# Block products of a feed-forward layer on one core: the split of the next pair's weight sums placed behind the copies of this pair's partial sums on ScalarE

## The chip, the cores and the metric

The kernel runs on one core of a Trainium2 chip. The metric is the device time of one execution in microseconds (us). Three runs of the kernel before took 1837.56, 1838.80 and 1840.89 us, median 1838.8. The core's engines work side by side, each through its own list of instructions in order: TensorE (PE, matmuls; PEld its weight loads), VectorE (DVE), ScalarE (ACT), GpSimd (POOL) and SyncE (SP, which here only issues DMA transfers). They wait for each other on semaphores.

## The reference

The kernel computes a trunk of two layers on 512 tokens of width 1024. Each layer has three attention mixers in parallel, a gated merge, and a feed-forward part; the modulation (shift, scale, gate) comes from a condition vector `c` by a product with `w_ada`.

```python
for l in range(DEPTH):
    mod = (cond @ w_ada[l] + b_ada[l]).reshape(b, 6, d)
    sh_a, sc_a, gt_a, sh_f, sc_f, gt_f = [mod[:, i, None, :] for i in range(6)]
    ...
    u = rms_norm(x, g_ffn[l]) * (1 + sc_f) + sh_f
    h = jax.nn.silu(u @ w_ffn_gate[l]) * (u @ w_ffn_up[l])
    x = x + gt_f * (h @ w_ffn_down[l])
return rms_norm(x, g_final)
```

All is float32. `D_FF` is 2816, that is 22 columns of 128. The change lies in the line that makes `h`.

## The kernel before, in words

**Split products.** TensorE multiplies in a short float format (`fp32r`). Each operand is split into a high part (a cast on ACT) and a low part (source less high part, on DVE), and every product is three matmuls: high by high, high by low, low by high (helper `mm3`, lines 225 to 227). So all weights pass from HBM into a raw tile (`wraw`, four buffers, line 173, issued by SP), through ACT's cast (line 196 for whole tiles `wh`, line 269 in `split`) and DVE's subtraction (line 198 for `wl`, line 270 in `split`).

**Pairs of block products.** Gate and up columns `f` = 0 to 2 are plain products. For `f` = 3 to 21 the two columns of a pair are cut into 2 x 2 blocks and computed by seven block products instead of eight, from sums of weight blocks and sums of activation blocks (`t1` to `t4`, made once). Each product is 12 matmuls of 256 columns. There are 19 such pairs in each of the two layers. TensorE's order is fixed by hand, and in pair `f` it is:

- y2 (`t2` by the pair's s24 sum, onto `y`), v1 (`t1` by s31, into `v`), p1 of the next pair (into the next `y`), y3 (`t3` by s31, onto `y`), v2 (onto `v`, by s24), p2 of the next pair (into `z`), y4 (`t4` by the plain weights, onto `y`).

`y`, `v` and `z` are PSUM tiles. Between products ACT copies the partial sum out: `kept_copy` (line 1035) makes the copy of `y` after p1 ("y1"), of `y` after y2 ("y2") and of `v` after v1 ("v1"). y3 goes on writing `y` and so waits for the y2 copy; v2 waits for the v1 copy; the next y2 waits for the y1 copy. y4 waits for DVE's sum u22 (line 1082), which reads `y` after y3.

**Weights of a pair.** A pair's weights are two raw tiles: `ra` (four blocks) and `rb`. `plain(f)` casts `ra` whole (`wh`) and half of `rb` (`a12h`), and fetches further loads. `sums(f)` adds blocks: s31 on DVE (line 1015), s24 in two sums on POOL (lines 1016 and 1017). `summed(f, i)` splits a sum: i = 0 gives s31h and s31l, i = 1 gives s24h and s24l. When the last reader of a raw tile is done, SP may issue the load that comes next in its order into that buffer.

**Background.** While the pairs run in layer 0, each odd pair asks for one `background` step: one column block of the next layer's `w_ada` is loaded into a `wraw` buffer and reduced against the condition vector by DVE (line 399). There are ten in layer 0 and one in layer 1. A finished pair's `h` column is stored to HBM (`h_kept`, line 930, issued by POOL) and read back for the down product.

**What sets the order.** On PE the order is as written. On ACT, DVE, POOL and SP a scheduler places the instructions by priority: recorded earlier means more urgent, and what stands under `high_priority` is taken as 30 steps more urgent. An order dependency without a semaphore (`add_manual_dep`) puts an instruction behind another on its engine.

The functions that the change touches, with the lines that the profile names:

Of the kernel before, what the change touches and what calls it, by code (L numbers as in the profile page):

```python
# [24 lines left out]
NF = FF // P  # L25
# [43 lines left out]
def tile_hybrid_trunk(ctx: ExitStack, tc: tile.TileContext, xT, cvec, pos, cst, cmask, vec, gfin,  # L69
                      w_ada, w_first, w_proj, w_uq, w_uqr, w_ukv, w_o, w_out, w_gu, w_dn, out):  # L70
    nc = tc.nc
    act, dve, pool, pe = nc.scalar, nc.vector, nc.gpsimd, nc.tensor
# [16 lines left out]
    def pst(tag, name):  # L89
        return ps.tile([P, S], F32, tag=tag, bufs=PB[tag], name=name)  # L90
# [6 lines left out]
    order = mybir.DependencyInfo(mybir.DependencyClass.NoSync, mybir.DependencyReason.SCHED_ONLY)  # L97
# [7 lines left out]
    def fn(*args, **kw):  # L105
        i = act.activation(*args, **kw).ins  # L106
        tc.add_manual_dep(i, phase["fence"].name, order, reason="table set")
        phase["now"].append(i)
# [67 lines left out]
    def fetch(r):  # L176
        while len(raws) < min(r, cap[0]):
            raws.append(load(*LOADS[len(raws)][1:]))
# [3 lines left out]
    def divide(want, after=None):  # L182

        while len(splits) < min(want, cap[0]):
            j = len(splits)
            fetch(j + 1)
            c = LOADS[j][2]
            p_, tag = wp, ""
            if LOADS[j][0][0] == "h":
                p_, tag = hroom[0], f"h{LOADS[j][0][2]}"  # L190
            elif fourth[0]:
                fourth[1] += 1
                if fourth[1] % 4 == 1:
                    p_, tag = fourth[0], "x"
            wh = p_.tile([P, D], F32R, tag="wh" + tag, name="wh")
            ins = [act.copy(wh[:, :c], raws[j][:, :c]).ins]  # L196
            wl = p_.tile([P, D], F32R, tag="wl" + tag, name="wl")
            ins.append(dve.tensor_sub(wl[:, :c], raws[j][:, :c], wh[:, :c].bitcast(F32)).ins)  # L198
            for i, a in zip(ins, after or ()):
                tc.add_manual_dep(i, a.name, order, reason="more urgent")  # L200
            splits.append((wh, wl))
# [62 lines left out]
        for _ in g:  # L264
            tick()

    def split(h, l, src, scale=None):
        if scale is None:
            act.copy(h, src)  # L269
            dve.tensor_sub(l, src, h.bitcast(F32))  # L270
        else:
            act.activation(h, src, AF.Copy, scale=scale)
            dve.scalar_tensor_tensor(l, src, scale, h.bitcast(F32), ALU.mult, ALU.subtract)
# [141 lines left out]
    def background(n):  # L415
        for _ in range(n):
            if pending:
                ada(*pending.pop(0))
# [4 lines left out]
    def values(ap, psv, name, got):  # L423

        vt = ap.tile([P, S], F32, tag="vt", name="vt" + name)
        act.copy(vt, psv)

        def rest():
            t = pst("mm", "vT" + name)
            for b in range(NB):  # L430
                pe.transpose(t[:, b * P : (b + 1) * P], vt[:, b * P : (b + 1) * P], identf)
            v = ap.tile([P, NB, 2, 2, 64], F32R, tag="vv", bufs=2, name="v" + name)
            tv = t.rearrange("p (b h f) -> p b h f", b=NB, h=2)
            split(v[:, :, :, 0], v[:, :, :, 1], tv)
            got.append(v)

        later(3, rest)
# [80 lines left out]
    for l in range(L):  # L518
# [32 lines left out]
        if l == 0:  # L551
            table(LN_EXP)
            st = su.enter_context(scoped("start"))
            t = pst("pt", "ssa0")
# [27 lines left out]
            def sums(c, after):  # L582
                return [ada(0, i, c, wada[c][i], i == 0, after[i]) for i in range(2)][1]
# [244 lines left out]
        for res, raw_, g0, tag in ((ckv, lat[3:], V_GKV, "ckv"), (cq, lat[:3], V_GQ, "cq")):  # L828
            for b in norms(tag + str(l), len(raw_) * P, latp):
# [4 lines left out]
                for i, t in enumerate(raw_):  # L834
                    rw, h, lo = t[:, b.cols], res[i][0][:, b.cols], res[i][1][:, b.cols]
# [9 lines left out]
        for w in range(1, 13):  # L845
# [12 lines left out]
            for a in range(2):  # L858
                h = 2 * w - 2 + a
# [17 lines left out]
        with scoped(f"mo{l}", "right") as op:  # L877
# [11 lines left out]
            for m in range(KC - NL):  # L889
                t = pst("mm", "wout")  # L890
# [6 lines left out]
            for b, tag in zip(both, ("mm", "s")):  # L897
                for i, w in enumerate(ws):
                    t = pst(tag, "wout")[:, :H]
# [29 lines left out]
        def kept(f, g):  # L929
            pool.dma_start(out=hsave[f], in_=g)  # L930
# [44 lines left out]
        for f in range(1, NSTD):  # L975
            if f == 1:
                t = ts[2]
            else:
                t = pst("mm", "fg")
# [14 lines left out]
        def half(hl, i):  # L994
            return [tuple(w[:, i * HC + k * P : i * HC + (k + 1) * P] for w in hl) for k in range(4)]

        def plain(f):

            j = first_of["ra", l, 2 * f]
            divide(j + 1)  # L1000
            fetch(j + 2)
            RA[f] = splits[j]
            h, lo = (gs.tile([P, HC], F32R, tag="a12" + a, bufs=2, name="a12" + a) for a in "hl")
            split(h, lo, raws[j + 1][:, HC:])
            A12[f] = h, lo
            splits.append(None)
# [10 lines left out]
            pool.tensor_add(s24[:, 1], s24[:, 0], rb[:, HC:])  # L1017
            sraw[f] = s31, s24

        def summed(f, i):  # L1020
            src = sraw[f][i].rearrange("p a c -> p (a c)")
            nm_ = ("s31", "s24")[i]
            h, lo = (gs.tile([P, D], F32R, tag=nm_ + a, bufs=1 + i, name=nm_ + a) for a in "hl")
            split(h, lo, src)
            SW[f, i] = h, lo

        def product(o, wt, acts, start):
            for k, ((wh, wl), (ah, al)) in enumerate(zip(wt, acts)):
                mm3(o, wh, wl, ah, al, start and k == 0, k == 3, not start)
# [2 lines left out]

        def kept_copy(name, src):
            t = gs.tile([P, H], F32, tag=name, name=name)
            act.copy(t, src)
            return t

        def p1(f):
            Y[f] = pst("mm", "y")[:, :H]
            product(Y[f], half(RA[f], 0), B[0, 0], True)  # L1040
            with tc.high_priority(offset=HP):
                Y1[f] = kept_copy("y1", Y[f])

        def p2(f):
            z = pst("s", "z")[:, :H]
            product(z, half((A12[f][0], A12[f][1]), 0), B[1, 0], True)
            G[f] = tp.tile([P, S], F32, tag="g", bufs=3, name="g")
            with tc.high_priority(offset=HP):
                dve.tensor_add(G[f][:, HALVES[0]], z, Y1[f])

        plain(NSTD)
        sums(NSTD)
        summed(NSTD, 1)
        summed(NSTD, 0)
        plain(NSTD + 1)
        p1(NSTD)
        p2(NSTD)
        for f in range(NSTD, NF):
            if f + 1 < NF:
                sums(f + 1)  # L1060
                summed(f + 1, 1)
            if f + 2 < NF:
                plain(f + 2)
            if f == NF - 1:
                at[0] = first_of["h", l, 0]
                cap[0] = first_of["h", l, 2]
                divide(cap[0])
            background(f % 2)
            y_, g = Y[f], G[f]
            product(y_, half(SW[f, 1], 0), TB["t2"], False)  # L1070
            with tc.high_priority(offset=HP):
                y2c = kept_copy("y2", y_)
            v = pst("pt", "v")[:, :H]
            product(v, half(SW[f, 0], 1), TB["t1"], True)
            with tc.high_priority(offset=HP):
                v1 = kept_copy("v1", v)
            if f + 1 < NF:
                p1(f + 1)
            product(y_, half(SW[f, 0], 0), TB["t3"], False)
            with tc.high_priority(offset=HP):  # L1080
                u22 = gs.tile([P, H], F32, tag="u22", name="u22")
                dve.tensor_add(u22, y_, v1)
            if f + 1 < NF:
                summed(f + 1, 0)
                fetch(first_of["ra", l, 2 * NSTD] + 2 * (f - NSTD) + 7)
            product(v, half(SW[f, 1], 1), B[1, 1], False)
            with tc.high_priority(offset=HP):
                dve.tensor_add(g[:, HALVES[1]], v, y2c)
                fn(g, g, AF.Silu)
            if f + 1 < NF:  # L1090
                p2(f + 1)
            product(y_, half(RA[f], 1), TB["t4"], False)
            with tc.high_priority(offset=HP):
                ga, gb = g[:, HALVES[0]], g[:, HALVES[1]]
                dve.scalar_tensor_tensor(gb, u22, -1.0, gb, ALU.mult, ALU.mult)
                dve.scalar_tensor_tensor(ga, y_, -1.0, ga, ALU.mult, ALU.mult)
                kept(f, g)
# [41 lines left out]
        for m in range(2, KC - 1):  # L1139
            t = pst("mm", "dn")  # L1140
# [6 lines left out]
        for b, tag in zip(both, ("mm", "s")):  # L1147
            t = pst(tag, "dn")[:, :H]
# [117 lines left out]
def _build(arrays):  # L1266
    import concourse.bacc as bacc

    nc = bacc.Bacc("TRN2", target_bir_lowering=False, num_devices=1)
    feeds, args = {}, []  # L1270
    for name, a in arrays.items():
        feeds[f"in_{name}_dram"] = a
        args.append(nc.dram_tensor(f"in_{name}_dram", a.shape, mybir.dt.from_np(a.dtype), kind="ExternalInput").ap())
    args.append(nc.dram_tensor("out_dram", (KC, P, S), F32, kind="ExternalOutput").ap())
    with tile.TileContext(nc) as tc:
        tile_hybrid_trunk(tc, *args)
    return nc, feeds
# [10 lines left out]
```

## Time and profile before

| | before |
|---|---|
| runs, us | 1837.56, 1838.80, 1840.89 |
| median, us | 1838.8 |
| profiled execution, its own time, us | 1839.1 |
| its span, us | 1837.3 |
| mean granted TensorE clock | 0.991 |
| PE busy, us (share of the span) | 1790.6 (97%) |
| DVE busy, us | 1398.3 (76%) |
| ACT busy, us | 965.5 (53%) |
| POOL busy, us | 281.0 (15%) |
| DMA, mean GB/s over the span | 135 |

The span is the time from the first to the last instruction in the profiled execution; the execution's own time is 1.8 us longer. Times in the trace count from the span's start. The block products of layer 0 lie at about 620 to 815 us, those of layer 1 at about 1517 to 1708. A row of the timeline gives start, duration, engine, line, operation and tiles, and in brackets how long the engine was idle before and what released it. Layer 0's pairs start at 619.66 (pair 3), 633.62 (pair 4), 643.30 (pair 5) and 653.13 (pair 6).

### The profile page before, as it was taken

The page shows a single profiled execution, that of the slowest core. Times are in us where ns is not written, and L with a number is a line of the kernel's source. Part 1 is how long each engine was busy: PE and PEld are TensorE (multiplying, and loading weights), DVE is VectorE, ACT ScalarE, POOL GpSimd, SP SyncE. Part 2 cuts the span into 40 slices and gives each one's busy share as a digit, 9 for nine tenths or more (in the row PEclk, how much of TensorE's full clock was granted, in tenths as well). Part 3 has the DMA queues.
Part 4 walks back from the last instruction along what each step waited for, and adds up shares of the span by engine and source line. Part 5 has one row for each costly group of instructions (what it writes and reads, how often), then busy time and mean ns, then how long its engine had stood idle before and what let it go on. Part 6 is the DMA issues. An engine that isn't in the chain of part 4 may idle for free.

```text
span 1837.3 us, 27818 instructions
## 1 busy us (share of the span) xinstructions
PE 1790.6 (97%) x10324; PEld 1552.4 (84%) x10324; DVE 1398.3 (76%) x2301; ACT 965.5 (53%) x1751; POOL 281.0 (15%) x398
## 2 busy tenths in 40 slices
PE   6999999999999999999999999999999999999997
PEld 4788888888889899988887887888888889999887
DVE  8888887778756899976568898877776588898533
ACT  4767884454335455553237688645433374555521
POOL 4122100001000233210002121000110013332000
PEclk8999999999999999999999999999999999999999
DMA  7423223434652455568644233343455324445631
GB/s 281 146 78 73 82 72 121 118 113 142 205 164 74 126 159 159 165 200 281 203 139 113 54 82 82 92 123 113 131 184 179 120 87 132 144 128 166 212 97 46
DMA packets 86263, 247.52 MB, mean 135 GB/s; under 512 B 11824, under 2 KB 15024, under 8 KB 86128
## 3 DMA queue, kind: packets, MB, share of 16 engines
q1 hardware_dynamic: 75120, 224.83, 39.5%
q0 software_dynamic: 11008, 20.92, 4.0%
q8 instruction: 81, 1.33, 0.3%
q14 instruction: 54, 0.44, 0.1%
HBM read 220.74 MB, written 15.73 MB: 129 GB/s over the span
## 4 chain that ended last, share of the span: by engine, by line
PE 78%; DVE 9%; DMA 5%; ACT 4%; issue 3%; POOL 1%; DVEq 0%; SPq 0%; ACTq 0%; POOLq 0%
PE gate L225 5%; PE gate L226 5%; PE gate L227 5%; PE proj L225 5%; PE proj L226 4%; PE proj L227 4%; PE y L225 3%; PE y L226 3%; PE y L227 3%; DMA wraw<-in_w_ada_dram 3%; PE o L225 2%; PE o L227 2%; PE o L226 2%; PE dn L226 2%; PE dn L225 2%
## 5 line engine op out<-in xcount | busy, mean ns | idle before, releaser
L196 ACT CAST wh<-wraw 128x1024 fp32r<-128x1024 f32 (+4 forms) x316 | 294.2, 934 | 317.3 <-PE dn L226 72.0
L198 DVE TENSOR_TENSOR wl<-wraw,wh 128x1024 fp32r<-128x1024 f32 (+4 forms) x316 | 362.3, 1150 | 119.2 <-ACT wh L196 112.9
L225 PE MATMUL proj<-uh,wh 128*128 128x512 f32 x384 | 161.1, 420 | 0.2
L225 PE MATMUL gate<-uh,wh 128*128 128x512 f32 x384 | 153.4, 400 | 0.0
L226 PE MATMUL proj<-ul,wh 128*128 128x512 f32 x384 | 151.2, 394 | 0.0
L227 PE MATMUL proj<-uh,wl 128*128 128x512 f32 x384 | 151.1, 393 | 0.0
L226 PE MATMUL gate<-ul,wh 128*128 128x512 f32 x384 | 150.2, 391 | 0.0
L227 PE MATMUL gate<-uh,wl 128*128 128x512 f32 x384 | 150.2, 391 | 0.0
L225 PE MATMUL dn<-wh 128*128 128x512 f32 (+1 forms) x396 | 145.1, 366 | 0.0
L226 PE MATMUL dn<-wl,wh 128*128 128x512 f32 (+1 forms) x396 | 145.0, 366 | 0.0
L227 PE MATMUL dn<-wh,wl 128*128 128x512 f32 (+1 forms) x396 | 144.8, 366 | 0.0
L399 DVE CUSTOM_DVE_ANT_0 wraw<-wraw,condb 128x1024 f32<-128x1024 f32 x80 | 97.5, 1219 | 48.0 <-DMA wraw<-in_w_ada_dram 48.0
L1016 POOL TENSOR_TENSOR s<-s,wraw 128x512 f32<-128x512 f32 x38 | 49.3, 1298 | 246.5 <-ACT a12h L269 166.8
L227 PEld LDWEIGHTS proj<-uh,wl 128*128 128x128 f32 x384 | 72.4, 188 | 16.7
L227 PEld LDWEIGHTS gate<-uh,wl 128*128 128x128 f32 x384 | 72.1, 188 | 15.9
L226 PEld LDWEIGHTS dn<-wl,wh 128*128 128x128 f32 x396 | 74.7, 189 | 12.6 <-DVE wl L198 0.7
L227 PEld LDWEIGHTS dn<-wh,wl 128*128 128x128 f32 x396 | 74.7, 189 | 12.3 <-DVE wl L198 0.2
L225 PEld LDWEIGHTS dn<-wh 128*128 128x128 f32 x396 | 74.7, 189 | 12.2
L225 PEld LDWEIGHTS gate<-uh,wh 128*128 128x128 f32 x384 | 72.2, 188 | 12.9
L226 PEld LDWEIGHTS gate<-ul,wh 128*128 128x128 f32 x384 | 72.3, 188 | 12.5
L106 ACT ACTIVATE lefts<-ss 128x512 f32<-128x512 f32 (+1 forms) x64 | 28.1, 439 | 100.5 <-DVE ss L450 85.6
L225 PEld LDWEIGHTS proj<-uh,wh 128*128 128x128 f32 x384 | 72.7, 189 | 9.1 <-PE sm L746 0.8
(443 smaller groups left out, 5364.5 us busy)
## 6 DMA issues: line engine op xcount, KB each, us to landing
wraw<-in_w_proj_dram SPq DMA_DIRECT2D x96, 512.0 KB, 3.7
wraw<-in_w_gu_dram SPq DMA_DIRECT2D x88, 512.0 KB, 3.7
wraw<-in_w_ada_dram SPq DMA_DIRECT2D x80, 512.0 KB, 3.5
wraw<-in_w_dn_dram SPq DMA_DIRECT2D x32, 512.0 KB, 4.3
wraw<-in_w_o_dram SPq DMA_DIRECT2D x48, 256.0 KB, 2.6
h_kept<-g POOLq DMA_DIRECT2D x44, 256.0 KB, 5.0
wraw<-h_kept SPq DMA_DIRECT2D x22, 512.0 KB, 4.9
wada<-in_w_ada_dram SPq DMA_DIRECT2D x16, 512.0 KB, 5.4
```

Source lines behind the costliest of these rows:

```text
L106: i = act.activation(*args, **kw).ins
L196: ins = [act.copy(wh[:, :c], raws[j][:, :c]).ins]
L198: ins.append(dve.tensor_sub(wl[:, :c], raws[j][:, :c], wh[:, :c].bitcast(F32)).ins)
L225: pe.matmul(o, wh, ah, start=start, stop=False, skip_group_check=again)
L226: pe.matmul(o, wh, al, start=False, stop=False, skip_group_check=again)
L227: pe.matmul(o, wl, ah, start=False, stop=stop, skip_group_check=again)
L399: ins = dve.tensor_tensor_reduce(out=wt, in0=wt, in1=condb, op0=ALU.mult, op1=ALU.add, scale=1.0, scalar=0.0, accum_out=m).ins
L1016: pool.tensor_add(s24[:, 0], s31[:, 1], ra[:, :HC])
```

## The change

`split` gets an argument `after`: an instruction behind which ACT's cast is placed by an order dependency. `kept_copy` records its copies in a list. In the loop over the pairs, the split of the next pair's s24 sum (`summed(f + 1, 1)`) and the plain weights of the pair after (`plain(f + 2)`) are recorded no longer at the start of the pair but behind the copy of v1, and the split's cast is tied behind that copy. `background(f % 2)` stays where it was and so is now recorded ahead of `plain(f + 2)`.

```diff
-    def split(h, l, src, scale=None):
+    def split(h, l, src, scale=None, after=None):
         if scale is None:
-            act.copy(h, src)
+            i = act.copy(h, src).ins
+            if after:
+                tc.add_manual_dep(i, after.name, order, reason="more urgent")
             dve.tensor_sub(l, src, h.bitcast(F32))
...
-        def summed(f, i):
+        def summed(f, i, after=None):
...
-            split(h, lo, src)
+            split(h, lo, src, after=after)
             SW[f, i] = h, lo
...
         def kept_copy(name, src):
             t = gs.tile([P, H], F32, tag=name, name=name)
-            act.copy(t, src)
+            copies.append(act.copy(t, src).ins)
             return t
+
+        copies = []
...
         for f in range(NSTD, NF):
             if f + 1 < NF:
                 sums(f + 1)
-                summed(f + 1, 1)
-            if f + 2 < NF:
-                plain(f + 2)
             if f == NF - 1:
...
             with tc.high_priority(offset=HP):
                 v1 = kept_copy("v1", v)
+            if f + 1 < NF:
+                summed(f + 1, 1, copies[-1])
+            if f + 2 < NF:
+                plain(f + 2)
             if f + 1 < NF:
                 p1(f + 1)
```

The order on TensorE is the same in both programs. The other engines differ in the two feed-forward stages alone. The lines of the changed kernel are up to five higher: 1035 becomes 1037, 270 becomes 272, 399 becomes 401, 1082 becomes 1087.

On ACT, pair 4 of layer 0. The copies read y2's `y`, v1's `v` and p1's `y`, in this order. Before:

```order
L106 ACTIVATE g<-g 128x512
L269 CAST a12h<-wraw 128x512
L196 CAST wh<-wraw 128x1024
L269 CAST s24h<-s_6446 128x1024
L1035 COPY y_6476<-y 128x256
L1035 COPY v_6491<-v 128x256
L1035 COPY y_6506<-y 128x256
L269 CAST s31h<-s_6445 128x1024
```

and with the change:

```order
L106 ACTIVATE g<-g 128x512
L269 CAST a12h<-wraw 128x512
L196 CAST wh<-wraw 128x1024
L1037 COPY y_6462<-y 128x256
L1037 COPY v_6477<-v 128x256
L269 CAST s24h<-s_6446 128x1024
L1037 COPY y_6506<-y 128x256
L269 CAST s31h<-s_6445 128x1024
```

The cast of the s24 sum moved from ahead of the copies of y2 and v1 to behind both. In the first pair of a layer the cast `a12h` stands between the two copies, and the cast `wh` of `ra` of pair 5 ahead of the copy of p1's `y`, before and now.

On SP, the loads of layer 0's feed-forward stage, from its start: six plain tiles (`f` = 0 to 2), then `ra` and `rb` of pairs 3, 4, 5 and so on, and the ada columns. Before:

```order
L173 DMA wraw<-in_w_gu_dram 128x1024 x12
L173 DMA wraw<-in_w_ada_dram 128x1024
L173 DMA wraw<-in_w_gu_dram 128x1024 x4
L173 DMA wraw<-in_w_ada_dram 128x1024
L173 DMA wraw<-in_w_gu_dram 128x1024 x4
```

and with the change:

```order
L173 DMA wraw<-in_w_gu_dram 128x1024 x10
L173 DMA wraw<-in_w_ada_dram 128x1024
L173 DMA wraw<-in_w_gu_dram 128x1024 x5
L173 DMA wraw<-in_w_ada_dram 128x1024
L173 DMA wraw<-in_w_gu_dram 128x1024 x4
```

The first ada column moved ahead of the two loads of pair 5; the next ones stand between `ra` and `rb` of pairs 7, 9 and so on, and no longer ahead of an `ra`.

On DVE, pair 4 of layer 0. `ISA wraw,mod_81` is the reduction of an ada column, `u_` is u22, `L1015` and `L1017` the s31 sum. Before, this pair had no ada column (pair 5 had, at the same place):

```order
L198 TENSOR_TENSOR wl<-wraw,wh 128x1024
L270 TENSOR_TENSOR s24l<-s_6446,s24h 128x1024
L1082 TENSOR_TENSOR u_6520<-y,v_6491 128x256
L270 TENSOR_TENSOR s31l<-s_6445,s31h 128x1024
L1088 TENSOR_TENSOR g<-v,y_6476 128x256
```

and with the change:

```order
L198 TENSOR_TENSOR wl<-wraw,wh 128x1024
L272 TENSOR_TENSOR s24l<-s_6446,s24h 128x1024
L401 ISA wraw,mod_81<-wraw,condb 128x1024
L401 ISA mod_81 128x1
L1087 TENSOR_TENSOR u_6520<-y,v_6477 128x256
L272 TENSOR_TENSOR s31l<-s_6445,s31h 128x1024
L1093 TENSOR_TENSOR g<-v,y_6462 128x256
```

The reduction of each ada column from the second on moved one pair ahead, from odd into even pairs, where it stands before u22 as it did. The load that it reads waits in the changed program for the second sum on POOL (line 1019 there) of the same pair, and before for the first sum (line 1016).

## The prediction

> **What bounds the kernel now.** First the page's busy table and chain of waits.
>
> ```profile
> PE 1790.6 (97%) x10324; PEld 1552.4 (84%) x10324; DVE 1398.3 (76%) x2301; ACT 965.5 (53%) x1751; POOL 281.0 (15%) x398
> PE 78%; DVE 9%; DMA 5%; ACT 4%; issue 3%; POOL 1%; DVEq 0%; SPq 0%; ACTq 0%; POOLq 0%
> ```
>
> TensorE (PE) is the bound. The change leaves its order as it is, so it can only shorten or lengthen the moments in which TensorE waits. Second, the table by stretches: from the first pair of block products to the start of the last one, in layer 0 and layer 1, then single pairs (columns: length, busy us of PE, PEld, DVE, ACT, POOL, granted clock, DMA share, GB/s).
>
> ```profile
> 619.66:805.39 185.73, 180.61 (x1514) 179.19 (x1513) 170.10 (x211) 93.46 (x144) 58.03 (x54) 0.98 0.53 161
> 1517.30:1698.45 181.15, 178.12 (x1515) 177.51 (x1513) 161.32 (x186) 93.84 (x144) 58.03 (x54) 0.99 0.45 142
> 619.66:633.62 13.96, 11.43 (x86) 11.23 (x85) 10.96 (x16) 4.58 (x8) 4.39 (x4) 0.88 0.46 131
> 633.62:643.30 9.68, 9.68 (x86) 9.68 (x85) 8.48 (x10) 5.22 (x8) 2.81 (x4) 1.00 0.47 138
> 653.13:663.10 9.97, 9.97 (x86) 9.89 (x85) 9.07 (x12) 5.72 (x9) 3.35 (x4) 1.00 0.46 131
> 791.13:805.39 14.26, 11.68 (x86) 11.44 (x85) 10.73 (x15) 6.02 (x9) 3.47 (x3) 0.88 0.59 190
> 1517.30:1531.30 14.00, 11.56 (x86) 11.36 (x85) 11.00 (x16) 4.57 (x8) 4.42 (x4) 0.88 0.40 132
> ```
>
> Each of the first two rows holds 18 pairs. A pair without a wait takes 9.68 us (fourth row), 18 of them 174.24. So the excess is 185.73 - 174.24 = 11.49 us in layer 0 and 181.15 - 174.24 = 6.91 in layer 1: 18.4 us is all that an order of ScalarE (ACT) can win here. Layer 0's first pair holds 4.28 of it, its next to last one 4.58, layer 1's first 4.32; the rest is 2.63 in layer 0 and 2.59 in layer 1. Third, TensorE's waits:
>
> ```profile
> PE y L225 <- ACT y L1035: 5.6, 4, 2.5
> PE v L225 <- ACT v L1035: 2.6, 1, 2.6
> ```
>
> The large waits are for the copies that the change lets pass ahead. Each is followed by a stretch at a lower clock: the three pairs with a wait of about 2.5 us have a mean clock of 0.88, so the wait costs 4.3 to 4.6 in all. A wait of 1.55 us elsewhere left it alone:
>
> ```profile
> 988.64 0.47 PE L702 MATMUL sf<-t,t 128*128 128x512 f32 x1 [1.55 <-DMA t<-t]
> 985.00:992.00 7.00, 5.45 (x27) 4.28 (x26) 6.00 (x14) 5.68 (x13) 1.02 (x2) 1.00 0.41 112
> ```
>
> So idle time costs its own length up to at least 1.55 us, and by 2.5 us some 1.7 more.
>
> **Part 1, the first pair of each layer.** Layer 0:
>
> ```profile
> 613.51 2.56 SPq L173 DMA_DIRECT2D wraw<-in_w_gu_dram  x2
> 618.17 1.05 ACT L196 CAST wh<-wraw 128x1024 fp32r<-128x1024 f32 x1
> 619.12 0.35 ACT L1035 COPY y<-y 128x256 f32<-128x256 f32 x1
> 619.66 0.28 PE L225 MATMUL y<-t2h,s24h 128*128 128x256 f32 x1
> 622.39 0.33 SPq L173 DMA_DIRECT2D wraw<-in_w_ada_dram  x1
> 624.62 1.04 ACT L269 CAST s24h<-s 128x1024 fp32r<-128x1024 f32 x1 [5.14 <-POOL s L1017]
> 626.09 0.37 ACT L1035 COPY y<-y 128x256 f32<-128x256 f32 x1
> 626.51 0.58 PE L225 MATMUL y<-t3h,s31h 128*128 128x256 f32 x1 [2.53 <-ACT y L1035]
> wraw<-in_w_gu_dram SPq DMA_DIRECT2D x1, 512.0 KB, 3.9
> ```
>
> ACT waits 5.14 us for GpSimd's (POOL) sums before the s24 cast, and the y2 copy stands behind it, so the third product waits 2.53. The change takes that away. But the ada column of the next layer takes the slot of the first of the two loads at 613.51 and `ra` of pair 5 the second, at 613.51 + 2.56 - 0.33 = 615.74 (an issue takes 0.33, fifth row). The cast of `ra` stands ahead of the copy of p1's sum. With the 3.9 of the last row (the second load's own) it lands at 619.66, cast 1.05 and copy 0.35 end at about 621.0: y2, due at 619.66, waits 1.35. `rb` of pair 5 then takes the slot that the ada load had at 622.39, lands 3.6 to 3.9 later, and its a12 cast stands ahead of the v1 copy: some 0.45 more for v2, and 0.5 for small waits behind both. Pair: 9.68 + 1.35 + 0.45 + 0.5 = 12.0 instead of 13.96, **-2.0 in each layer**; bounds -4.3 (no wait left) and 0.
>
> **Part 2, the small waits of the middle pairs.** Pair 6 shows them and the timing of the rest:
>
> ```profile
> 654.56 1.36 POOL L1017 TENSOR_TENSOR s<-s,wraw 128x512 f32<-128x512 f32 x1
> 655.86 0.56 POOL L930 DMA_DIRECT2D h_kept<-g  x1
> 655.95 1.05 ACT L269 CAST s24h<-s 128x1024 fp32r<-128x1024 f32 x1 [0.64 <-POOL s L1017]
> 656.91 0.36 ACT L1035 COPY y<-y 128x256 f32<-128x256 f32 x1
> 657.33 0.39 PE L225 MATMUL y<-t3h,s31h 128*128 128x256 f32 x1
> 659.10 0.42 DVE L1082 TENSOR_TENSOR u<-y,v 128x256 f32<-128x256 f32 x1 [0.36 <-issue]
> 661.67 0.28 PE L225 MATMUL y<-t4h,wh 128*128 128x256 f32 x1
> ```
>
> The copy ends at 657.27, 4.14 after the pair's start at 653.13, and y3 starts when it is there: this pair took 9.97 instead of 9.68. With the copies first there is no such wait: -2.6 in layer 0, and in layer 1 about -2.0 (I leave 0.6 of its 2.59 for its last pair, where the casts of the kept products come in). The moved cast ends at about pair start + 4.3 and its low part on VectorE (DVE) at + 5.5; both are read only in the next pair, so they cost nothing. Bounds: 0 and -5.2 for both layers.
>
> **Part 3, what the moved `plain` brings with it: the ada column in layer 0.** `background` now comes before `plain(f+2)`, so the ada load stands on SyncE's (SP) queue between `ra` and `rb` of a pair, in every even pair, and takes the slot that POOL's second sum frees. Its reduction stands on DVE ahead of that pair's u22 sum; y4's first matmul waits for u22, because u22 reads the PSUM tile that y4 goes on writing. Before, the load went out one sum earlier in an odd pair, here pair 5, which starts at 643.30:
>
> ```profile
> 644.53 0.33 SPq L173 DMA_DIRECT2D wraw<-in_w_ada_dram  x1
> 648.68 1.22 DVE L399 CUSTOM_DVE_ANT_0 wraw<-wraw,condb 128x1024 f32<-128x1024 f32 x1
> 645.97 10.31 SPq L173 DMA_DIRECT2D wraw<-in_w_gu_dram  x4
> wraw<-in_w_ada_dram SPq DMA_DIRECT2D x1, 512.0 KB, 3.5
> wraw<-in_w_gu_dram SPq DMA_DIRECT2D x1, 512.0 KB, 5.5
> h_kept<-g POOLq DMA_DIRECT2D x1, 256.0 KB, 5.1
> ```
>
> The load issued at 644.53 takes 3.5 (fourth row, of that moment alone) and is there at 648.0, when DVE comes to its reduction at 648.68 without a wait. The fifth row is the last load of the third: issued at 645.97 + 10.31 - 0.33 = 655.95, the end of pair 6's second sum, just the place in question. The load of `ra` is still under way then, and the store of the sixth row leaves in the same moment. The ada load inherits this place, so I take 5.5. Issue at pair start + 2.8 (655.95 - 653.13), landing at + 8.3, reduction 1.2, u22 0.42: u22 ends at about + 9.9. y4 is due at 661.67 - 653.13 less the 0.3 that this pair lost = + 8.25. TensorE waits 1.6 to 1.7 us; I take **1.6**, and 0.25 more for what follows a wait (in pair 6 the first matmul takes 0.39 instead of 0.28, and the pair lost 0.29 in all to a wait too short to show): 1.85 in each of pairs 4, 6, ... 18, **8 x 1.85 = +14.8**. In pair 6 now u22 ends 2.15 before y4 (659.52 against 661.67): that is the cover used up. What queues behind the waiting reduction on DVE are u22, s31's low part, g's sum with y2, and the next pair's s31 sum; they all move with y4. Bounds: with 3.5 instead of 5.5 u22 ends at + 7.9 and the wait is gone (0); at 5.5 with every wait long enough to lower the clock, 8 x (1.85 + 1.7) = +28.
>
> [...]
>
> **Part 4, the end of the stage.**
>
> ```profile
> 798.13 1.04 ACT L269 CAST s24h<-s 128x1024 fp32r<-128x1024 f32 x1 [4.73 <-POOL s L1017]
> 799.50 0.39 PE L225 MATMUL v<-uh,s24h 128*128 128x256 f32 x1 [2.58 <-ACT v L1035]
> ```
>
> Here too copies wait behind the cast, and pass it now. But the sums are as late as before (4.73), and u22 and the casts of the kept products follow. I keep 3.5 of the 4.58: **-1.0** in layer 0 and 0 in layer 1 (bounds -4.6 and +2).
>
> **Sum.** Layer 0: -2.0 - 2.6 + 14.8 - 1.0 = +9.2. Layer 1, where only the first pair has an ada column: -2.0 - 2.0 = -4.0. Together +5.2. The profiled execution took 1839.1, so 1844.3; the median of the runs lies 0.3 lower, so **1844 us**.
>
> **The rivals.** (1) *Faster: the ada load lands in time.* The same terms without part 3's +14.8: -9.6, so 1829. For it: the load's own 3.5 now. Against it: that is at another moment, and the load that holds this place now takes 5.5. It decides from a latency below 8.25 - 0.42 - 1.2 - 2.8 = 3.8 us. (2) *No difference: half a wait.* The ada load has `ra` beside it for only a part of its way and lands in about 4.6: a wait of 0.7 + 0.25, 8 x 0.95 = 7.6, against -9.6: 1837. For it: it is the middle between 3.5 and 5.5. Against it: in pair 6 the same company, `ra` and the store, is there from the first moment. (3) *Much slower: the clock falls at every wait.* 1.7 more for each of the 8, so 1858. For it: 2.5 us did it three times, and 1.6 is just above the longest wait (1.55) that I know to be harmless. [...] (4) *The change does not do what it says*: the built order shows the casts behind both copies in every pair, so next to nothing.
>
> **Chances.** Forecast 0.57 (its own range 1840 to 1849), rival 1 0.14, rival 2 0.17, rival 3 0.10, else 0.02. What a measurement of this kernel can tell from no change is about 0.2%, 3.7 us: 1835.1 to 1842.5. Of the forecast 0.10 lies within that, 0.47 above; of rival 2 0.12 lies within and 0.05 below. Slower: 0.47 + 0.10 + 0.02 = 0.59; same 0.22; faster 0.14 + 0.05 = 0.19. The range of 8 in 10 leaves out two thirds of rivals 1 and 3 (0.16) and a few hundredths else: 1831 to 1856.
>
> **What would show it.** In the changed profile: no wait of PE y for the y copy of 2.5 us after the first pair's start; the granted clock near 1.00 there; a new row in TensorE's waits, y4 for DVE's u22, 8 or 9 times at about 1.6 in layer 0 and none in layer 1; before each, DVE idle until the ada load lands, and that load taking about 5.5. Even pairs of layer 0 take 11.5, odd ones 9.68, those of layer 1 all 9.68. It is wrong if the ada load lands within 4 us (then faster), if the clock shows 0.88 in the even pairs, or if the first pairs still take 14.

## The result and the profile after

The changed kernel takes 1851.13 us (median of 8 runs, 1846.20 to 1860.01) against 1839.49 for the kernel before (8 runs beside them, 1836.58 to 1842.65). The ratio is 1.0063, with a 95% interval of 1.0043 to 1.0083: slower, by 11.6 us. The forecast was 1844, slower by 5.2; the measured time lies above the forecast's own range of 1840 to 1849 and within its 1831 to 1856. The execution that was profiled is one of the shorter ones: 1848.04 us, span 1846.3.

The same table by stretches as in the prediction, of the changed kernel (length, busy us of PE, PEld, DVE, ACT, POOL, granted clock, DMA share, GB/s): all 18 pairs of layer 0 and of layer 1, then pairs 3, 4, 5, 6 and 8 of layer 0 and pair 3 of layer 1.

```profile
619.48:817.52 198.04, 182.22 (x1513) 180.06 (x1513) 169.24 (x208) 93.59 (x144) 57.70 (x54) 0.97 0.48 150
1532.55:1707.39 174.84, 174.84 (x1513) 174.68 (x1513) 161.55 (x183) 95.03 (x144) 57.69 (x54) 1.00 0.47 146
619.48:629.74 10.26, 10.24 (x84) 10.05 (x85) 9.01 (x12) 3.81 (x7) 3.82 (x3) 1.00 0.57 179
629.74:642.47 12.73, 9.95 (x86) 9.75 (x85) 9.62 (x13) 4.83 (x9) 3.19 (x3) 1.00 0.44 119
642.47:652.15 9.68, 9.68 (x86) 9.68 (x85) 9.68 (x13) 6.09 (x10) 3.16 (x3) 1.00 0.53 172
652.15:663.62 11.47, 9.93 (x86) 9.73 (x85) 8.90 (x13) 4.34 (x8) 3.17 (x3) 1.00 0.46 131
673.30:686.02 12.72, 10.75 (x86) 10.55 (x85) 9.75 (x13) 5.05 (x8) 3.17 (x3) 0.93 0.45 139
1532.55:1542.68 10.13, 10.13 (x84) 10.05 (x85) 9.01 (x12) 3.81 (x7) 3.82 (x3) 1.00 0.59 183
```

Layer 1 got what the split promised: 174.84 us where 181.15 stood, 0.6 above 18 undisturbed pairs of 9.68. Layer 0 went the other way: 198.04 instead of 185.73. TensorE's waits, their largest rows on the pairs:

```profile
PE y L225 <- DVE u L1087: 15.8, 10, 2.8
...
PE y L225 <- ACT y L1037: 2.8, 2, 1.4
```

The waits for ACT's copies inside the pairs are gone. The second row is the wait for the y1 copy ahead of each first pair, 1.4 us, which the prediction put at 1.35. The first row is new: ten waits for u22, eight of them, 15.0 us, in pairs 4 to 18 of layer 0. Pair 6 (from 652.15) shows the chain, on SP, then DVE, then PE:

```profile
655.10 0.33 SPq L173 DMA_DIRECT2D wraw<-in_w_ada_dram  x1
...
656.69 1.21 DVE L272 TENSOR_TENSOR s24l<-s,s24h 128x1024 fp32r<-128x1024 f32 x1
660.47 1.22 DVE L401 CUSTOM_DVE_ANT_0 wraw<-wraw,condb 128x1024 f32<-128x1024 f32 x1 [2.57 <-DMA wraw<-in_w_ada_dram]
...
661.62 0.42 DVE L1087 TENSOR_TENSOR u<-y,v 128x256 f32<-128x256 f32 x1
...
662.10 0.38 PE L225 MATMUL y<-t4h,wh 128*128 128x256 f32 x1 [1.54 <-DVE u L1087]
```

The ada load leaves at pair start + 2.95, in the moment in which POOL's second sum is done. DVE, whose next instructions stand in order behind the reduction, is idle for 2.57 us, and y4 waits 1.54. The transfers issued in that moment, with their time to landing:

```profile
wraw<-in_w_ada_dram SPq DMA_DIRECT2D x1, 512.0 KB, 5.2
h_kept<-g POOLq DMA_DIRECT2D x1, 256.0 KB, 4.8
```

In the other even pairs up to 18 the ada load took 5.4 to 5.8.

Where the difference lies, by terms (us; each is a difference of stretches of the two profiles):

| term | forecast | measured |
|---|---|---|
| first pairs of both layers, with the wait ahead of them | -4.0 | -4.8 |
| pairs 4 to 18 of layer 0 | +12.2 (14.8 - 2.6) | +19.3 |
| pairs 19 and 20 of layer 0 | -1.0 | -3.3 |
| pairs 4 to 20 of layer 1 | -2.0 | -2.4 |
| sum | +5.2 | +8.8 |

The two profiled executions differ by 1848.04 - 1839.1 = 8.9. Outside the pairs they differ by -1.6 ahead of layer 0's pairs and +1.7 between the two layers' pairs, which cancel. Each goes with one stretch of 3.41 us at half clock that only one of the two profiles has: at 90.22 us in the one before, at 1001.62 in the changed one.

### The profile page after: what moved, and what is told of

It is laid out like the page before. It is cut to its first block, busy times and chain, and to the rows that moved or that the text cites. A ratio compares the mean times of both kernels' runs of the same rounds, so it can differ in the third digit from the quotient of the medians.

```text
span 1846.3 us, 27812 instructions
## 1 busy us (share of the span) xinstructions
PE 1788.6 (97%) x10324; PEld 1550.3 (84%) x10324; DVE 1402.1 (76%) x2301; ACT 967.5 (52%) x1751; POOL 280.9 (15%) x398
## 5 line engine op out<-in xcount | busy, mean ns | idle before, releaser
L227 PEld LDWEIGHTS proj<-uh,wl 128*128 128x128 f32 x384 | 72.4, 188 | 16.7
```

The source lines that it names most:

```text
L227: pe.matmul(o, wl, ah, start=False, stop=stop, skip_group_check=again)
```

## Experiments

**The two halves of the edit, each alone.** The change does two things: the split of the s24 sum moves behind the copies, and `plain(f + 2)` moves with it, which puts the ada load between `ra` and `rb`.

The split alone (against the changed kernel):

```diff
             if f + 1 < NF:
                 sums(f + 1)
+            if f + 2 < NF:
+                plain(f + 2)
...
                 summed(f + 1, 1, copies[-1])
-            if f + 2 < NF:
-                plain(f + 2)
```

> The changed kernel with the plain weights of the pair after (and so the loads) recorded at the start of the pair again, as before: only the split of the s24 sum stands behind both copies, and the ada loads go out where they did. Theory A (the loss is the ada reduction that waits for its load ahead of u22, and the moved split alone is a gain): no wait for u22 in layer 0; first pairs about 9.8 us each (-4.2 twice), small waits of the middle pairs gone (-2.6 and -2.4), the end of layer 0 -3.3: about -16.7, so 1823 us. Rival B (the later split itself makes u22 late): waits of 1.6 us and more for u22 stay, 1846 or above.

Measured: 1831.77 us, ratio to the kernel before 0.9961 (0.9947 to 0.9974). The split alone makes the kernel faster, by 7.2 us; the forecast of 16.7 was more than twice that. Its profile: layer 0, layer 1, and pair 20 of layer 0.

```profile
617.69:801.34 183.65, 176.60 (x1514) 175.81 (x1513) 170.35 (x211) 95.12 (x144) 58.24 (x54) 0.99 0.52 164
1515.24:1691.12 175.88, 174.68 (x1514) 174.36 (x1513) 162.69 (x185) 95.39 (x144) 58.24 (x54) 1.00 0.47 146
785.01:801.34 16.33, 11.40 (x86) 11.01 (x85) 12.58 (x15) 7.35 (x11) 3.50 (x3) 0.90 0.53 177
```

Of the 9.4 us by which layer 0 exceeds 18 undisturbed pairs, 6.65 are in pair 20. There the end of the stage comes in, which looked better in the changed kernel and is worse here than before (16.33 against 14.26). Fifteen of the sixteen pairs between take 9.7. The waits for u22 are not all gone, as theory A had it: the first pairs took 11.08 and 11.15 us with waits of 1.0 and 1.2 for it, and pair 7 of layer 0 took 11.05 with one of 1.1. These and pair 20 are what the forecast missed.

The order of the loads alone (against the kernel before):

```diff
                 sums(f + 1)
                 summed(f + 1, 1)
-            if f + 2 < NF:
-                plain(f + 2)
...
                 v1 = kept_copy("v1", v)
+            if f + 2 < NF:
+                plain(f + 2)
```

> The kernel before with only the plain weights of the pair after recorded behind the copy of v1: the split of the s24 sum stands ahead of both copies as before, the ada load goes out between the two loads of a pair as in the changed kernel. Theory A: 8 waits for u22 of 1.6 to 3 us in layer 0 (+22 with the falls of the clock), the copies still late in the first pairs and at the end, the y1 copy late too: 1857 to 1865 us. Rival B: no wait for u22, about 1839.

Measured: 1855.18 us, ratio 1.0087 (1.0062 to 1.0112), 1.8 below the range of theory A (1857 to 1865) and far above rival B. Its layer 0 and its waits:

```profile
619.76:823.74 203.98, 181.20 (x1512) 177.29 (x1513) 170.89 (x211) 92.83 (x144) 57.81 (x54) 1.00 0.47 148
```

```profile
PE y L225 <- ACT y L1037: 12.4, 14, 1.4
...
PE y L225 <- DVE mod L405: 7.8, 5, 2.0
PE y L225 <- DVE u L1086: 5.6, 4, 1.7
```

The last two rows are the wait of y4 behind the reduction and u22, 13.4 us in all; the longest is 2.0, and no stretch of half clock lies in these pairs (granted clock 1.00), so theory A's 22 was too much. The first row shows that the old waits for the copies even grew: in pair 7, for one, ScalarE waits 1.12 us for the load of `rb` and then 0.70 for the s24 sum, and the copies stand behind both. So, each alone, the two halves are a gain of 7 us and a loss of 16. Their sum, 9, is 2.6 short of the 11.6 of both together; the falls of the clock in the changed kernel's pairs may be the reason, but no run shows that.

**Is it the place in VectorE's queue?** If y4 waits because u22 stands behind the reduction, u22 may go first.

```diff
-            background(f % 2)
+            background(f % 2, u22s[-1] if u22s else None)
...
-                dve.tensor_add(u22, y_, v1)
+                u22s.append(dve.tensor_add(u22, y_, v1).ins)
```

Here `background` hands the instruction on to `ada`, which places the reduction behind it by an order dependency.

> The changed kernel with each ada reduction placed behind the u22 sum of its pair by an order dependency on VectorE; loads and splits as in the changed kernel. Theory A (the place in VectorE's queue makes the loss): the load still takes 5.5 us and VectorE still waits for it, but TensorE does not wait for u22; first pairs as in the changed kernel (10.2 us and the 1.5 us ahead of them): about 1826 to 1830 us. Rival C (the order of the loads makes the weights late, wherever the reduction stands): new waits for the casts of ra, rb or for the s31 parts, 1840 or above.

Measured: 1849.13 us, ratio 1.0054 (1.0035 to 1.0073). Theory A missed by some 20 us. Waits on the pairs, then pairs 6 and 7 of layer 0:

```profile
PE y L225 <- DVE u L1087: 8.3, 8, 3.0
PE v L227 <- DVE s31l L272: 5.4, 7, 1.2
```

```profile
651.56:661.24 9.68, 9.68 (x87) 9.68 (x85) 7.33 (x9) 5.14 (x8) 3.18 (x3) 1.00 0.47 137
661.24:673.47 12.23, 10.64 (x86) 10.04 (x85) 11.66 (x16) 5.07 (x9) 3.58 (x3) 1.00 0.47 152
```

The even pair is free of waits, and the odd pair behind it takes 12.23. VectorE still stood idle for the load, so it had done only 7.33 us of work in the even pair and makes up 11.66 in the next: s31's low part comes late, then the next u22. The wait moved and kept its price: pairs 4 to 18 of layer 0 take 162.73 us here (629.77 to 792.50), 14.9 more than before; in the changed kernel they waited 15.0 for u22.

That gave a second theory, D: VectorE is nearly full in these pairs. Pairs 4 to 18 of layer 0, before and with the change:

```profile
633.62:781.45 147.83, 147.82 (x1263) 146.84 (x1261) 140.10 (x172) 77.84 (x120) 47.21 (x46) 1.00 0.52 159
```

```profile
629.74:796.86 167.12, 152.09 (x1262) 150.52 (x1261) 140.85 (x174) 78.15 (x121) 47.55 (x45) 0.97 0.46 142
```

```profile
DVE wraw L401 <- DMA wraw<-in_w_ada_dram: 23.0, 8, 3.2
```

Before, VectorE worked 140.10 us of 147.83; 7.7 us were free. With the change it does the same work (140.85) and stands idle for 23.0 us behind eight ada loads (third row, of the changed kernel in these pairs). What doesn't fit into the free time, some 15 us, TensorE has to wait for, at both places in the queue that were measured.

**Take the idle time away, and leave the loads where they are.** The reduction goes behind the gate products that finish the pair, into the next pair, when its data have long landed.

```diff
-            background(f % 2)
+            background(f % 2, gates[-1] if gates else None)
...
-                dve.scalar_tensor_tensor(ga, y_, -1.0, ga, ALU.mult, ALU.mult)
+                gates.append(dve.scalar_tensor_tensor(ga, y_, -1.0, ga, ALU.mult, ALU.mult).ins)
```

> The changed kernel with each ada reduction placed behind the gate products (line 1101) that finish the pair before, so about 2 us into the next pair, when its load has long landed; the order of the loads and of ScalarE's copies stays the changed one. Theory D (VectorE is nearly full in these pairs, about 1 us free in two of them; it is the 2.6 to 3.1 us in which it stands idle for the load that TensorE pays for, and putting u22 ahead of the reduction only moved the bill to s31's low part and the next u22): no idle time on VectorE for the load, no waits for u22 in pairs 4 to 18, about 1826 to 1830 us. Rival C (the order of the loads itself is the harm, since rb of a pair now waits until the reduction has freed its buffer): new waits for a12 or the sums, 1838 or above.

Measured: 1829.01 us, ratio 0.9952 (0.9936 to 0.9968). Layer 0 and the reductions in it (the last two numbers are VectorE's idle time ahead of them):

```profile
621.90:799.44 177.54, 175.03 (x1513) 174.64 (x1513) 165.45 (x205) 94.24 (x143) 57.56 (x54) 1.00 0.52 167
```

```profile
L401 DVE CUSTOM_DVE_ANT_0 wraw<-wraw,condb 128x1024 f32<-128x1024 f32 x9 | 17.9, 1985 | 0.0
```

The idle time is 0.0, every pair from 4 to 19 takes 9.7, and the loads are those of the changed kernel, so rival C (the order of the loads harms by itself) is out. A reduction at this place even takes 1.99 us instead of 1.22 (why is open), and no pair from 4 to 19 is longer for it. Pair 20 of layer 0 takes 12.74.

**The end of the stage.** In the split-only profile ScalarE waited ahead of the s31 cast of the next to last pair:

```profile
784.21 1.05 ACT L196 CAST wh<-wraw 128x1024 fp32r<-128x1024 f32 x1 [4.10 <-DMA wraw<-h_kept]
785.16 1.05 ACT L269 CAST s31h<-s 128x1024 fp32r<-128x1024 f32 x1
```

The cast of a kept tile, needed only in the down product, stands ahead of a cast that TensorE needs at once. Edit: the first two kept tiles are split behind the last s31 split (`s31s` holds the cast and the subtraction of each s31 split).

```diff
-                divide(cap[0])
+                divide(cap[0], s31s[-1])
```

> The split-only kernel with the casts and low parts of the first two tiles of kept products placed behind the split of the last pair's s31 sum (order dependencies on ScalarE and VectorE). In the split-only profile the next to last pair of layer 0 took 16.33 us, because ScalarE waited 4.10 us for a kept tile ahead of the s31 cast. If that is the cause the pair takes 9.7 to 10.5 and the kernel 1825 to 1826 us; if VectorE's lag comes from the ada reduction there, it stays at 13 or more and the kernel at 1829 to 1832.

Measured: 1827.83 us, ratio 0.9948 (0.9932 to 0.9964), 3.9 us less than the split alone by the two medians, where 6 were expected. But the kernel before, run beside each, was 2.1 us faster this time (1836.85 against 1838.95), and the intervals of the two ratios, 0.9961 and 0.9948, overlap: the medians alone don't show a gain. The profile does. Pair 20 takes 9.68 (176.40 us for layer 0 instead of 183.65), so the kept tiles were in the way. TensorE's waits there had been 1.3 us for s31's low part and 3.7 for u22, which stood on VectorE behind the low part of the second kept tile; the edit moves casts and low parts together and doesn't tell which of them counted more. The first pair of layer 1 took 1.1 us more in that execution.

> As the one before, and the first ada reduction of each layer stands behind u22 of the first pair. In the split-only profile the first pairs took 11.07 and 11.14 us with a wait for u22 behind that reduction. By theory D VectorE has room there only if it stood idle for other reasons: 9.9 to 10.5 in the first pairs, 1.0 to 2.4 us less in all, 1823 to 1825. If VectorE is full there too, the wait moves to pair 4 and nothing is gained.

Here the first reduction of each layer is recorded behind u22 of its pair:

```diff
-            background(f % 2)
+            if f > NSTD:
+                background(f % 2)
...
+            if f == NSTD:
+                background(1, u)
```

Measured: 1826.94 us, ratio 0.9943 (0.9928 to 0.9959). The first pairs take 9.79 and 9.78 us. But pair 4 takes 10.30 and 10.31 and pair 5 of layer 0 10.56: most of the gain came back as waits of up to 0.6 us, as theory D has it. Against the run before it this is no difference that can be told. Its median is the lowest of this study, 0.57% below the kernel before and 1.2% below the changed one.

**When does the clock fall?** In the changed kernel's profile pairs 8, 12 and 16 lost 1.7 us more than the others to a stretch at half clock, with waits of 2.0 to 2.2 us, while pair 4 waited 2.8 without one. The next run is a kernel with waits of many lengths (the u22 sum repeated, on the split-only kernel; `behind` keeps VectorE's other work of the pair behind the repeats; those lines are left out here):

```diff
-                dve.tensor_add(u22, y_, v1)
+                reps = (6, 7, 8, 9, 10, 11, 12, 14)
+                k = (f - 4) // 2
+                n = reps[k if l == 0 else 7 - k] if f % 2 == 0 and f < 20 else 1
+                for _ in range(n):
+                    last[0] = dve.tensor_add(u22, y_, v1).ins
```

> The split-only kernel, in which VectorE repeats the u22 sum 6, 7, 8, 9, 10, 11, 12, 14 times in pairs 4, 6, ... 18 of layer 0, and in the reverse order in layer 1: y4 then waits between about 0.7 and 3.5 us by design (about 0.36 us for each repeat beyond 4). It asks when TensorE's clock falls. Rival L (by the length alone): every wait above some 2.0 us is followed by half clock for about 3 us (+1.7), every shorter one is not, in both layers alike. [...] Total: 16 waits of 2.0 on the mean, +33, and 4 to 10 falls, +7 to +17, above the split-only kernel.

Measured: 1913.06 us, much more than planned, since a repeat cost 0.46 us instead of 0.36 and VectorE's lag carried over into the odd pairs: y4's waits in the even pairs were 1.0 to 5.9 us. Pair 6 of layer 0 (a wait of 3.4 us), pair 12 of layer 1 (2.1) and, with half clock, pair 8 of layer 0 (4.6):

```profile
649.99:663.59 13.60, 10.22 (x86) 9.96 (x85) 12.83 (x18) 6.31 (x10) 3.52 (x3) 1.00 0.43 136
1672.08:1684.12 12.04, 9.93 (x86) 9.73 (x85) 11.52 (x19) 5.42 (x8) 3.04 (x3) 1.00 0.36 110
673.86:689.56 15.70, 11.12 (x86) 10.93 (x85) 14.28 (x21) 6.18 (x10) 3.52 (x3) 0.83 0.36 118
```

The first two waits, 3.4 and 2.1 us, left the clock at 1.00, which rival L doesn't allow. As a scale of lengths the run is too coarse; the same pairs in another execution tell more. So the changed kernel was profiled twice more, unaltered.

> The changed kernel, unaltered, profiled once more. In its first profile three of the eight waits in even pairs of layer 0 (2.1 to 2.3 us) were followed by half clock, and one of 2.95 was not. Rival L (the length decides): the waits recur with the same lengths and the same three pairs, 8, 12 and 16, are followed by half clock. [...]

> [...]

Measured: 1849.87 and 1855.08 us.

| profile of the changed kernel | time, us | even pairs of layer 0 followed by half clock |
|---|---|---|
| first | 1848.04 | 8, 12, 16 |
| second | 1849.87 | 6, 16 |
| third | 1855.08 | 4, 10, 14, 16 |

Other pairs fall each time. The waits did not recur with the same lengths (pair 6 waited 1.54, 1.83 and 1.10 us in the three, pair 16 2.00, 2.59 and 2.50), but their lengths don't decide: 1.76 (pair 14, third profile) and 1.83 (pair 6, second) were followed by half clock, 2.44 (pair 4, second) and 2.79 (pair 4, first) were not. So rival L is out. The count of falls doesn't give the time either: the second profile has one fall less than the first and is 1.8 us longer. The first four rows are two of the four falls of the third profile, each behind the stretch just ahead of it; the fifth is a stretch with a wait of 1.97 us that no half clock followed:

```profile
640.50:643.90 3.40, 1.70 (x13) 1.70 (x14) 3.33 (x6) 0.26 (x1) 0.00 (x0) 0.98 0.30 75
643.90:647.10 3.20, 3.20 (x16) 3.20 (x16) 3.20 (x5) 2.02 (x4) 2.13 (x2) 0.50 0.22 87
705.20:708.60 3.40, 1.56 (x14) 1.41 (x12) 3.03 (x6) 0.00 (x0) 0.00 (x0) 1.00 0.24 36
708.60:712.00 3.40, 3.40 (x19) 3.40 (x18) 3.40 (x6) 2.07 (x3) 2.03 (x2) 0.50 0.30 118
728.15:731.50 3.35, 1.38 (x12) 1.18 (x11) 2.72 (x5) 0.00 (x0) 0.00 (x0) 1.00 0.24 26
```

The trace also records when the granted clock changes. The four falls of this profile begin at 643.76, 708.61, 752.98 and 776.88 and last 3.41 us each.

## Why the prediction was right or wrong

**What bounds, and part 1.** Right. TensorE's order stayed and only its waits moved. In the first pairs both mechanisms came as worked out: the 2.5 us wait for the y2 copy went, the y1 copy came 1.4 us late behind the cast of `ra` (forecast 1.35). The gain was 2.3 and 2.5 us where 2.0 was forecast, since the pair itself lost 0.6 and 0.45 us where the forecast had 0.95 for the late v1 copy and what follows it.

**Part 2.** Right: with the ada loads out of the way (the split alone) all middle pairs but one take 9.7, and in layer 1 the sum came to -2.4 against -2.0.

**Part 3.** The step decided the sign and its chain was right: the load takes 5.2 to 5.8 us at this place (forecast 5.5, from the load that held it before) where it took 3.5, the reduction waits, y4 waits for u22. The size was short: pairs 4 to 18 came out 7.1 us above the forecast. Of this, three falls of the clock are 5.1 (3 x 1.7). The rest, about 2, is pair 4, where the load left 3.7 us after the pair's start (633.40 against 629.74) instead of 2.8, and the three pairs that fell, whose waits were 2.0 to 2.2 instead of 1.6; the other four lost 1.7 to 1.95 in all, against 1.85. Two sentences of the step mislead. That what queues behind the waiting reduction moves with y4 is true, but it made the place ahead of u22 look like the cause; and the 2.15 us that u22 had in pair 6 before were not the cover that counted: with u22 put first the loss remained at 10 us. What was used up was VectorE's free time, 0.5 us a pair.

**Part 4.** Too small: -3.3 instead of -1.0. In the changed kernel the last ada columns are loaded and reduced earlier; in the split alone they aren't, and the next to last pair took 16.33. That points to the early ada loads, but no run shows it alone: the kernel that put the reduction a pair later has the same order of loads, and its pair 20 took 12.74, against 10.31 in the changed kernel and 14.26 before. So the cause of this gain stays open.

**The sum and the rivals.** Forecast +5.2, in the profiles +8.8, in the medians +11.6: the direction and the mechanism were right, the size was less than half. That the profiles come as near as 3.6 us is in part luck, since part 3 came out 7.1 too small and the other terms 3.5 too careful. Rival 1 (the load lands in 3.5) and rival 2 (half a wait) did not come. Rival 3, the falling clock, had been taken for all or nothing, with a chance of 0.10. It came in part, in 2 to 4 of 8 pairs in each of the three profiles. That was the step that failed: a sharp bound between 1.55 us (harmless) and 2.5 (not), where the runs show none in the length of the wait: in the three profiles 1.76 us was followed by half clock and 2.79 was not. It may be one reason for the spread of the changed kernel's runs, 13.8 us against 6.1 of the kernel before. The mean granted clock of the eight runs goes with their time, 0.991 in the three shortest (1846 to 1848 us) and 0.988 in the longest (1860), but 0.003 of 1850 us is only some 5.5. What made the median's further 2.8 us stays open.

## What to carry to other kernels

A moved line moves everything that it issues, and everything recorded next to it: here the aim of the change was a cast on ScalarE, worth 7 us, and most of its cost comes from a load that changed places on another engine's queue. Before a load is put just ahead of its use, look at how full the consuming engine is: VectorE, 95% busy in these pairs and not the bound, could not stand still for 2.9 us in every second pair, at either of the two places in its queue, without TensorE paying. Let such an engine read what has long landed, as in the kernel that put the reduction a pair later: the same loads, the same work, about 20 us less than the changed kernel (ratios 0.9952 and 1.0063 to the kernel before).

## What the runs showed of the hardware

TensorE's clock fell to half behind some waits and not behind others, and the length of the wait didn't decide which. In the three profiles of the changed kernel, pairs 4 to 18 of layer 0, nine waits for u22 were followed by a stretch at half clock:

| profile of the changed kernel | followed by half clock: wait, us (pair) | not followed, the longest: wait, us (pair) |
|---|---|---|
| first | 1.97 (8), 2.18 (12), 2.00 (16) | 2.79 (4) |
| second | 1.83 (6), 2.59 (16) | 2.44 (4) |
| third | 2.30 (4), 1.84 (10), 1.76 (14), 2.50 (16) | 1.97 (12) |

Each stretch of the first and the third profile lasted 3.41 us. In the run with the repeated sums the waits of 3.38 us (pair 6 of layer 0) and 2.11 (pair 12 of layer 1) left the clock at 1.00, and that of 4.58 (pair 8 of layer 0) went with 0.83 over its pair. What decides whether a wait is followed by half clock was not shown by any run here.
